# Depthwise taps of the second layer's conv branch: six per projection over the first seven heads, the rest handed out at the merges from the third on

## The chip, the core and the metric

The kernel runs on one core of a Trainium2 chip. Times are device microseconds of one execution. Engines are named as in the profile: PE is TensorE, DVE is VectorE, ACT is ScalarE, POOL is GpSimd, SP is SyncE, which issues the DMAs here.

## What is computed

Two layers of a hybrid block over 256 latent tokens and 256 context tokens, width 1024, in fp32. Of one layer, the part that matters here, with h the normalised and modulated input:

```
q, k, v = h @ w_q, h @ w_k, h @ w_v            # 8 heads, two 64-wide halves each; 2-D rotary on q and k
p   = softmax(q k^T / 8)                       # for each half, keys = context + latent (512)
o   = (p[0] - lam * p[1]) @ v
y_b = rms_norm(o, subln_g) * c @ w_attn_out    # per head
u   = (h @ w_a) * sigmoid(h @ w_b)             # 512 channels
u   = depthwise_conv(u, width 31) + bias
y_a = silu(layer_norm(u)) @ w_conv_out
y_c = group_mix(window_means(h @ w_p) - h @ w_p) @ w_pool_out
y   = (g0 * y_a + g1 * y_b + g2 * y_c) @ w_out     # g = sigmoid(h @ w_g + b), three branches
```

then the residual and a SwiGLU feed-forward part. The second layer's context rows are not needed, so there the queries, the conv branch and the pooling run for the 256 latent tokens alone, and keys and values for 512.

## The kernel before

Activations lie channel by channel, 128 channels on the partitions and the tokens along the row. Each fp32 product is three matmuls on TensorE (lines 341 to 343): high part times high part, low times high, high times low. The weights come in units of 128 x 1024; SP loads a unit (`raw`, line 305), ACT makes its high part (`hi`, line 357) and DVE its low part (`lo`, line 358). Activations are split likewise (H, V, A, QH and QL).

The program is written in one order, and a scheduler that models times decides from it in which order each engine gets its instructions; the written order serves as priority. The engines then run their own lists strictly in order and wait for each other by semaphores.

The second layer's token mixer, in the written order:

- `glu` computes u. `conv_tasks` then makes a list of 124 small tasks, `self.bg`, 31 for each chunk of 128 channels. For chunks 0, 1 and 2 they run on DVE: one start (line 909) and 30 taps, each a multiply-add of a shifted row of u into the chunk's sum, O (line 930, 128 x 241 to 255). For chunk 3 a tap is a multiplication on ACT (line 925) and an addition on POOL (line 927). A POOL task stands behind every third DVE tap.
- `step(n)` takes the next n tasks off the list and writes them at this point of the program; `drain()` writes all that are left.
- The first half of the V projection, then eight heads. For each head comes the projection of Q and that of K, each followed by `rope_split`: a copy out of PSUM to T on ACT (line 705), on DVE a shuffle into sh and a multiplication by the cosine (707, 708), on POOL the multiplication by the sine (710), on DVE the sum (711). For Q, four DMAs copy T to QD (line 731), and ACT and DVE split it (QH, QL). For K, ACT makes two copies (line 720) and POOL the two low parts (line 721). Behind each of the 16 projections stands a `step(16)`, so that the list was empty after the eighth.
- Behind a head's projections stand the scores and products of the head before it (`head`): score matmuls (line 800, into pss), the largest element on DVE (803), the exponential on ACT (806), the reciprocal and the difference of the two softmaxes on DVE (810 to 813), transposes on PE (831, into pst), the split into A (357 and 358), the products with V (into pso), a copy to O on ACT (844). Ahead of head 4 stands the second half of the V projection.
- Heads 0 to 3 go through `subln` in the loop, heads 4 to 7 behind it: squares on ACT (855), a mean on PE (856), a root on ACT (860), a reciprocal on DVE (861), a broadcast on PE (869, 870).
- Ahead of the second `subln` stand the pooling projections with `pool_group` on POOL (lines 1000 to 1022), behind it the merges: for each branch eight gate projections with the products of that branch, branch 1 (attention) first, then 2 (pooling), then 0 (conv). `norm` (lines 937 to 964), the layernorm over the four conv chunks, is put on the list ahead of the merges; its result is needed in the merges of branch 0 alone.

Of the kernel before, what the change touches and what calls it, by code (L numbers as in the profile page):

```python
# [38 lines left out]
NH = 8  # L39
# [173 lines left out]
class Net:  # L213
# [815 lines left out]
    def layer(self, l, H, acts, first, xin, xnext, tail):  # L1029
        nc = self.nc  # L1030
        need_ctx = l < DEPTH - 1
# [7 lines left out]
        def os_to_yb(h0, h1):  # L1039
            yb.extend(self.subln(os[h0:h1], sg, n))  # L1040
# [13 lines left out]
        for h in range(NH):  # L1054
            if h == 4:
                V1 = self.v_proj(l, 1, acts)
            qk = []
            for col, sc, m in ((COL_Q, HD ** -0.5, n), (COL_K, 1.0, NT)):
                u = self.unit("in", l, col + h * P)
                ps = self.ps("g")  # L1060
                self.gemm_cm(ps[:, :m], u, acts, 0, m)
                qk.append(self.rope_split(ps, sc, m, col == COL_K,
                                          nc.vector if need_ctx else nc.gpsimd))
                self.step(self.S_QK)
            if pend is not None:
                os.append(self.head(l, *pend, lam, need_ctx))
                if len(os) == 4:
                    os_to_yb(0, 4)
            pend = (h, qk[0], qk[1], V if h < 4 else V1)
            if h % 2 == 0 and fill:  # L1070
                self.mod_block(l, fill.popleft(), bank=self.H_BK)
        os.append(self.head(l, *pend, lam, need_ctx))

        if need_ctx:
            us = self.glu(l, acts, n)
            taps, norm = self.conv_tasks(l, us, nseq, ya)
        else:
            self.drain()


        pooled = []
# [11 lines left out]
        def merge(branch, n_, yact, u_y, base):  # L1093
            t = self.M_BK[n_ % 2]
            pg, py = self.ps(t), self.ps(t)
            u = self.unit("in", l, COL_G + branch * D + n_ * P)
            self.gemm_cm(pg[:, :n], u, acts, 0, n)
            u_y = self.unit(*u_y) if u_y is not None else self.last_u
            self.last_u = u_y
            self.gemm_cm(py[:, :n], u_y, yact, 0, n, base)  # L1100
            gs = self.c2("S")
            nc.scalar.activation(gs[:, :n], pg[:, :n], AF.Sigmoid,
                                 bias=prm[:, O_BG + branch * 8 + n_:
                                          O_BG + branch * 8 + n_ + 1])
            if branch == 1:
                m = self.cn("O", n)
                nc.vector.tensor_tensor(out=m[:, :n], in0=py[:, :n], in1=gs[:, :n],
                                        op=ALU.mult)
                ms.append(m)
            else:  # L1110
                m = ms[n_]
                nc.vector.tensor_tensor(out=gs[:, :n], in0=py[:, :n], in1=gs[:, :n],  # L1112
                                        op=ALU.mult)
                nc.gpsimd.tensor_tensor(out=m[:, :n], in0=m[:, :n], in1=gs[:, :n],  # L1114
                                        op=ALU.add)
            if branch == 0:
                hi, lo = self.pair("V", n)
                self.split(hi[:, :n], lo[:, :n], m[:, :n])
                mhl.append((hi[:, :n], lo[:, :n]))

        for n_ in range(KC):
            merge(1, n_, yb, ("ao", l, n_), 0)
            self.step(self.S_B)


        hi, lo = self.unit("grp", l)
# [262 lines left out]
```

## Time and profile before

| | before |
|---|---|
| three runs | 1535.64, 1538.06, 1538.65 us, median 1538.06 |
| the profiled execution's own time | 1536.55 us |
| its span | 1534.6 us |
| PE busy | 1498.8 us, 98% |
| DVE busy | 997.5 us, 65% |
| ACT busy | 821.0 us, 53% |
| POOL busy | 343.0 us, 22% |
| mean granted clock of TensorE | 0.992 of its higher level |

The span is the time between the first and the last instruction of the profiled execution; its own time is 2 us longer and lies 1.5 us under the median. Times in rows are counted from the start of the span; the second layer's heads lie between about 1035 and 1200.

### The profile page before, as it was taken

The numbers are of one execution on the slowest core, as the hardware profiler recorded it, in microseconds if no ns is written. First come the engines' busy times: TensorE is split into PE (matmuls) and PEld (weight loads), VectorE is DVE, ScalarE is ACT, GpSimd is POOL, SyncE is SP. The second block draws the span as 40 slices with busy tenths as digits, with TensorE's granted clock in tenths as the row PEclk, the third lists the DMA queues.
The fourth block names the chain that finished last, engine by engine and source line by source line (L and its number), as shares of the span: only waits on it lengthen the run. The fifth ranks groups of instructions, "written<-read, shape, count | busy, mean of one in ns | idle before, by whom it ended". The sixth has DMA issues, their size and how long they took to land.

```text
span 1534.6 us, 22266 instructions
## 1 busy us (share of the span) xinstructions
PE 1498.8 (98%) x8310; PEld 1250.9 (82%) x8310; DVE 997.5 (65%) x1561; ACT 821.0 (53%) x1383; POOL 343.0 (22%) x320
## 2 busy tenths in 40 slices
PE   6999999999999999999999999998999999899998
PEld 3788878878877787888888888887879899799986
DVE  4587786999974337344444332799999656655544
ACT  5467667532344336454545453774668665644443
POOL 0010100540131100054554543053225312000000
PEclk9999999999999999999999999999999999999999
DMA  9552342133237643335435667333143567366553
GB/s 350 183 155 73 124 138 69 70 105 115 98 102 243 213 147 110 124 125 178 165 127 173 208 210 253 130 118 122 58 145 109 176 202 242 125 196 209 182 189 110
DMA packets 85148, 236.68 MB, mean 154 GB/s; under 512 B 10032, under 2 KB 15792, under 8 KB 85040
## 3 DMA queue, kind: packets, MB, share of 16 engines
q1 hardware_dynamic: 85040, 235.26, 45.9%
q8 instruction: 65, 1.06, 0.3%
q14 instruction: 43, 0.35, 0.1%
HBM read 223.69 MB, written 5.24 MB: 149 GB/s over the span
## 4 chain that ended last, share of the span: by engine, by line
PE 83%; DVE 11%; ACT 3%; issue 2%; DMA 0%; SPq 0%; POOL 0%; DVEq 0%; ACTq 0%
PE psg L341 14%; PE psg L342 13%; PE psg L343 13%; PE pss L343 10%; PE pss L342 10%; PE pss L341 10%; DVE O L930 3%; PE pso L342 2%; PE pso L341 2%; PE pso L343 2%; DVE lo L358 2%; DVE Q L930 2%; PE pss L800 2%; PE pss L392 1%; PE pst L831 1%
## 5 line engine op out<-in xcount | busy, mean ns | idle before, releaser
L358 DVE TENSOR_TENSOR lo<-raw,hi 128x1024 fp32r<-128x1024 f32 x299 | 385.3, 1290 | 244.2 <-ACT hi L357 236.2
L357 ACT ACTIVATE hi<-raw 128x1024 fp32r<-128x1024 f32 x299 | 315.0, 1056 | 411.1 <-PE psg L342 165.7
L341 PE MATMUL psg<-H,hi 128*128 128x512 f32 (+1 forms) x864 | 300.6, 349 | 2.3 <-ACT H L357 1.9
L342 PE MATMUL psg<-H,hi 128*128 128x512 f32 (+1 forms) x864 | 300.7, 348 | 0.7 <-DVE H L358 0.7
L343 PE MATMUL psg<-H,lo 128*128 128x512 f32 (+1 forms) x864 | 300.9, 349 | 0.0
L341 PE MATMUL pss<-H,hi 128*128 128x256 f32 (+1 forms) x704 | 234.9, 335 | 2.9 <-ACT H L357 2.8
L343 PE MATMUL pss<-H,lo 128*128 128x256 f32 (+1 forms) x704 | 236.2, 336 | 0.0
L342 PE MATMUL pss<-H,hi 128*128 128x256 f32 (+1 forms) x704 | 235.7, 335 | 0.0
L473 POOL TENSOR_TENSOR ma<-ma,mt 128x512 f32<-128x512 f32 x91 | 133.2, 1481 | 246.8 <-ACT mt L469 245.7
L341 PEld LDWEIGHTS psg<-H,hi 128*128 128x128 f32 x864 | 163.5, 190 | 28.6 <-issue 3.7
L343 PEld LDWEIGHTS psg<-H,lo 128*128 128x128 f32 x864 | 163.7, 189 | 23.8 <-issue 2.9
L342 PEld LDWEIGHTS psg<-H,hi 128*128 128x128 f32 x864 | 163.7, 189 | 23.7 <-issue 1.9
L341 PEld LDWEIGHTS pss<-H,hi 128*128 128x128 f32 x704 | 132.8, 189 | 17.7 <-ACT H L357 3.0
L342 PEld LDWEIGHTS pss<-H,hi 128*128 128x128 f32 x704 | 133.3, 190 | 15.7 <-DVE H L358 0.2
L343 PEld LDWEIGHTS pss<-H,lo 128*128 128x128 f32 x704 | 134.1, 191 | 13.9
L930 DVE SCALAR_TENSOR_TENSOR Q<-Q,perm,Q 128x482 f32<-128x482 f32 (+14 forms) x120 | 99.0, 825 | 2.5
L710 POOL TENSOR_TENSOR sh<-sh,perm 128x256 f32<-128x256 f32 x32 | 27.8, 868 | 260.5 <-DVE sh L707 189.4
L1114 POOL TENSOR_TENSOR O<-O,S 128x512 f32<-128x512 f32 (+1 forms) x32 | 43.3, 1355 | 184.7 <-DVE S L1112 184.7
L806 ACT ACTIVATE E<-pss,st 128x512 f32<-128x512 f32 (+1 forms) x96 | 58.7, 613 | 36.1 <-DVE st L803 30.7
L469 ACT ACTIVATE mt<-mr,perm 128x512 f32<-128x512 f32 x91 | 61.6, 715 | 21.4 <-DMA mr<-wmod 21.4
L1182 DVE TENSOR_TENSOR S<-pss,S 128x256 f32<-128x256 f32 (+1 forms) x43 | 23.9, 555 | 74.2 <-PE pss L343 72.0
L341 PE MATMUL psg<-V,hi 128*128 128x512 f32 (+1 forms) x192 | 64.7, 342 | 1.2 <-ACT S L860 1.2
(388 smaller groups left out, 2773.3 us busy)
## 6 DMA issues: line engine op xcount, KB each, us to landing
raw<-w SPq DMA_DIRECT2D x297, 512.0 KB, 3.4
mr<-wmod SPq DMA_DIRECT2D x72, 256.0 KB, 4.2
mod<-wmod SPq DMA_DIRECT2D x24, 512.0 KB, 5.2
A<-wmod SPq DMA_DIRECT2D x18, 256.0 KB, 5.1
O<-wmod SPq DMA_DIRECT2D x16, 256.0 KB, 5.8
QD<-T SPq DMA_DIRECT2D x32, 128.0 KB, 2.4
E<-wmod SPq DMA_DIRECT2D x14, 256.0 KB, 5.4
xs<-Q SPq DMA_DIRECT2D x12, 256.0 KB, 2.0
```

Of the source, the lines that this page charges most:

```text
L341: mm(out, sh, mh, start=start, stop=False)
L342: mm(out, sh, ml, start=False, stop=False)
L343: return mm(out, sl, mh, start=False, stop=stop)
L357: return (self.nc.scalar.activation(hi, src, AF.Copy), (lo_eng or self.nc.vector).tensor_tensor(out=lo, in0=src, in1=hi.bitcast(F32), op=A ...
L358: (lo_eng or self.nc.vector).tensor_tensor(out=lo, in0=src, in1=hi.bitcast(F32), op=ALU.subtract))
L469: nc.scalar.activation(t, src, AF.Copy, scale=self.cc[:, k, v:v + 1])
L473: nc.gpsimd.tensor_tensor(out=accs[v], in0=accs[v], in1=t, op=ALU.add)
L710: nc.gpsimd.tensor_tensor(out=sh, in0=sh, in1=self.sin, op=ALU.mult)
L800: nc.tensor.matmul(pss[j][:, :n], q[a][:, j, qt * P:(qt + 1) * P], k[:, j, k0:NT], start=(a == 0), stop=(a == 1))
L806: nc.scalar.activation(e[:, :n], pss[j][:, :n], AF.Exp, bias=mx[:, j:j + 1], accum_out=ss[:, j:j + 1])
L930: last[0] = nc.vector.scalar_tensor_tensor(out=av, in0=uv, scalar=prm[:, w:w + 1], in1=av, op0=ALU.mult, op1=ALU.add)
L1114: nc.gpsimd.tensor_tensor(out=m[:, :n], in0=m[:, :n], in1=gs[:, :n], op=ALU.add)
```

## The change

In the second layer each of the fourteen projections of heads 0 to 6 is followed by six tasks instead of sixteen, and those of head 7 by none. The call that wrote the rest of the list behind the last head is removed. The 40 tasks that are then left are handed out, ten at a time, behind the merges of branch 1 from the third on, with `norm` behind them. The first layer's program stays as it was, since its list is empty in the loop over heads and all its merges keep their step.

```diff
--- before.py
+++ after.py
@@ -1061,7 +1061,7 @@
                 self.gemm_cm(ps[:, :m], u, acts, 0, m)
                 qk.append(self.rope_split(ps, sc, m, col == COL_K,
                                           nc.vector if need_ctx else nc.gpsimd))
-                self.step(self.S_QK)
+                self.step(6 if h < NH - 1 else 0)
             if pend is not None:
                 os.append(self.head(l, *pend, lam, need_ctx))
                 if len(os) == 4:
@@ -1074,8 +1074,6 @@
         if need_ctx:
             us = self.glu(l, acts, n)
             taps, norm = self.conv_tasks(l, us, nseq, ya)
-        else:
-            self.drain()
 
 
         pooled = []
@@ -1120,7 +1118,8 @@
 
         for n_ in range(KC):
             merge(1, n_, yb, ("ao", l, n_), 0)
-            self.step(self.S_B)
+            if need_ctx or n_ > 1:
+                self.step(self.S_B)
 
 
         hi, lo = self.unit("grp", l)
```

All instructions stay the same; what changes is the order on each engine. Up to the end of the chunk 0 taps every engine has the order it had, chunk 3's taps on POOL included; PE has it again within the merges. Three places in between:

DVE at head 0. O_9232 is the sum of chunk 1 in the kernel before; V_9020 and the lo tiles belong to the V projection and to coming weight units, sh_9065 and T_9063 to head 0's Q, sh_9135 and T_9133 to its K. Before:

```order
L358 TENSOR_TENSOR V_9020<-pso_8886,V_9019 128x512
L930 SCALAR_TENSOR_TENSOR O_9232<-O_8685,perm,O_9232 128x243
L358 TENSOR_TENSOR lo_8908<-raw_8905,hi_8907 128x1024
L707 STREAM_SHUFFLE sh_9065<-T_9063 128x256
L930 SCALAR_TENSOR_TENSOR O_9232<-O_8685,perm,O_9232 128x244
L708 TENSOR_TENSOR T_9063<-T_9063,perm 128x256
L930 SCALAR_TENSOR_TENSOR O_9232<-O_8685,perm,O_9232 128x245
L711 TENSOR_TENSOR T_9063<-T_9063,sh_9065 128x256
L930 SCALAR_TENSOR_TENSOR O_9232<-O_8685,perm,O_9232 128x246
```

with taps between the remaining steps of head 0's K as well. After, where sh_9121 and T_9119 are head 0's K:

```order
L358 TENSOR_TENSOR V_9020<-pso_8886,V_9019 128x512
L358 TENSOR_TENSOR lo_8908<-raw_8905,hi_8907 128x1024
L707 STREAM_SHUFFLE sh_9065<-T_9063 128x256
L708 TENSOR_TENSOR T_9063<-T_9063,perm 128x256
L711 TENSOR_TENSOR T_9063<-T_9063,sh_9065 128x256
L358 TENSOR_TENSOR lo_9035<-raw_9032,hi_9034 128x1024
L707 STREAM_SHUFFLE sh_9121<-T_9119 128x256
L708 TENSOR_TENSOR T_9119<-T_9119,perm 128x256
L711 TENSOR_TENSOR T_9119<-T_9119,sh_9121 128x256
L358 TENSOR_TENSOR lo_9091<-raw_9088,hi_9090 128x1024
```

The taps of chunk 1, thirteen instructions from behind the last chunk 0 tap to the last rotation step of head 0's K, are gone from this place; they stand together with the rest of their chain in the second V projection. 

DVE from the last head's softmax to the second `subln`'s reciprocal (line 861, the last row of each). A is the split of the transposed weights of the last heads. Before:

```order
L810 RECIPROCAL st_10661<-st_10647 128x2
L811 TENSOR_TENSOR st_10661<-st_10661,perm 128x1
L813 SCALAR_TENSOR_TENSOR E_10637<-E_10637,st_10642,E_10640 128x512
L358 TENSOR_TENSOR A_10601<-pst_10595,A_10600 128x512
L813 SCALAR_TENSOR_TENSOR E_10656<-E_10656,st_10661,E_10659 128x512
L358 TENSOR_TENSOR A_10616<-pst_10610,A_10615 128x512
L358 TENSOR_TENSOR lo_10935<-raw_10932,hi_10934 128x1024
L358 TENSOR_TENSOR A_10672<-pst_10666,A_10671 128x512
L358 TENSOR_TENSOR A_10687<-pst_10681,A_10686 128x512
L358 TENSOR_TENSOR E_10738<-A_10728,E_10738 128x256
L358 TENSOR_TENSOR lo_10965<-raw_10962,hi_10964 128x1024
L861 RECIPROCAL S_10895<-S_10895 128x256
```

After, where O_10334 is the sum of chunk 2:

```order
L813 SCALAR_TENSOR_TENSOR E_10596<-E_10596,st_10601,E_10599 128x512
L930 SCALAR_TENSOR_TENSOR O_10334<-O_8816,perm,O_10334 128x248
L930 SCALAR_TENSOR_TENSOR O_10334<-O_8816,perm,O_10334 128x247
L930 SCALAR_TENSOR_TENSOR O_10334<-O_8816,perm,O_10334 128x246
L358 TENSOR_TENSOR A_10612<-pst_10606,A_10611 128x512
L930 SCALAR_TENSOR_TENSOR O_10334<-O_8816,perm,O_10334 128x245
L358 TENSOR_TENSOR A_10627<-pst_10621,A_10626 128x512
L930 SCALAR_TENSOR_TENSOR O_10334<-O_8816,perm,O_10334 128x244
L930 SCALAR_TENSOR_TENSOR O_10334<-O_8816,perm,O_10334 128x243
L930 SCALAR_TENSOR_TENSOR O_10334<-O_8816,perm,O_10334 128x242
L930 SCALAR_TENSOR_TENSOR O_10334<-O_8816,perm,O_10334 128x241
L861 RECIPROCAL S_10835<-S_10835 128x256
```

Taps of chunk 2 now stand between these steps: of the chain's 31 instructions, 25 lie between the two reciprocals of line 861, 21 of them ahead of the last split of A, and the chain ends right ahead of the second reciprocal. Before, no tap stood between the two. Two lo splits stand behind the reciprocal now.

PE at the products of the last head (into pso; A is the split of its transposed weights, psg_11104 the gate projection of the first merge). Before:

```order
L342 MATMUL psg_11104<-H_8340,hi_10837 128x256
L343 MATMUL psg_11104<-H_8338,lo_10838 128x256
L341 MATMUL psg_11104<-H_8338,hi_10837 128x256
L342 MATMUL psg_11104<-H_8340,hi_10837 128x256
L341 MATMUL pso_10627<-A_10671,V_9914 128x256
L342 MATMUL pso_10627<-A_10672,V_9914 128x256
L343 MATMUL pso_10627<-A_10671,V_9915 128x256
L341 MATMUL pso_10627<-A_10671,V_9918 128x256
```

After:

```order
L831 MATMUL pst_10606<-perm,E_10577 128x128
L831 MATMUL pst_10606<-perm,E_10596 128x128
L831 MATMUL pst_10621<-perm,E_10596 128x128
L831 MATMUL pst_10621<-perm,E_10577 128x128
L831 MATMUL pst_10621<-perm,E_10596 128x128
L341 MATMUL pso_10567<-A_10611,V_9799 128x256
L342 MATMUL pso_10567<-A_10612,V_9799 128x256
L343 MATMUL pso_10567<-A_10611,V_9800 128x256
```

The matmuls of the first merge that stood between the last transposes (line 831) and these products are drawn ahead; the products now follow the transposes directly.

## Rows read from the trace of the kernel before

**Rows 1.** The page of the profile, its first line and the line of part 1 on PE (busy us, share of the span, instructions of each engine).

```profile
span 1534.6 us, 22266 instructions
...
PE 1498.8 (98%) x8310; PEld 1250.9 (82%) x8310; DVE 997.5 (65%) x1561; ACT 821.0 (53%) x1383; POOL 343.0 (22%) x320
```

**Rows 2.** Waits of PE from 1040 to 1215 us, the three longest: who waited for whom, then us in total, times, longest.

```profile
PE pss L800 <- POOL K L721: 5.2, 1, 5.2
PE pso L856 <- ACT sq L855: 1.4, 1, 1.4
PE psg L341 <- ACT S L860: 1.2, 1, 1.2
```

**Rows 3.** Windows over the second layer's attention part: start and end, length; busy us and (instructions) of PE, PEld, DVE, ACT, POOL; granted clock of TensorE as a share of its higher level; busy share of the DMA engines; GB/s.

```profile
1054.10:1060.90 6.80, 5.64 (x15) 4.65 (x16) 6.76 (x10) 4.51 (x6) 3.24 (x3) 0.50 0.25 84
1060.90:1190.00 129.10, 128.01 (x759) 109.44 (x758) 124.60 (x238) 91.48 (x179) 45.78 (x52) 1.00 0.33 107
1197.50:1200.90 3.40, 3.40 (x17) 2.95 (x16) 2.39 (x4) 2.36 (x5) 0.00 (x0) 0.50 0.93 311
1220.00:1240.00 20.00, 20.00 (x167) 19.95 (x167) 13.73 (x20) 18.20 (x29) 0.00 (x0) 1.00 0.73 230
```

**Rows 4.** Timeline of PE ahead of the first score matmul: start, length, engine, line, operation, out<-in, count. The starts of neighbours show the pitch.

```profile
1049.71 0.28 PE L341 MATMUL psg<-H,hi 128*128 128x256 f32 x1
1049.83 0.28 PE L342 MATMUL psg<-H,hi 128*128 128x256 f32 x1
```

**Rows 5.** Timeline of DVE in the first V projection and at head 0 (and one row from the second V projection); several instructions of one kind in a row are one row with their count.

```profile
1019.40 3.15 DVE L930 SCALAR_TENSOR_TENSOR O<-O,perm,O 128x255 f32<-128x255 f32 x4
...
1035.84 0.93 DVE L930 SCALAR_TENSOR_TENSOR O<-O,perm,O 128x241 f32<-128x241 f32 x1
...
1038.02 0.45 DVE L930 SCALAR_TENSOR_TENSOR O<-O,perm,O 128x241 f32<-128x241 f32 x1
1038.40 1.21 DVE L358 TENSOR_TENSOR lo<-raw,hi 128x1024 fp32r<-128x1024 f32 x1
...
1042.04 0.43 DVE L707 STREAM_SHUFFLE sh<-T 128x256 f32<-128x256 f32 x1
...
1045.33 2.78 DVE L930 SCALAR_TENSOR_TENSOR O<-O,perm,O 128x246 f32<-128x246 f32 x4
...
1049.56 0.45 DVE L707 STREAM_SHUFFLE sh<-T 128x256 f32<-128x256 f32 x1
...
1052.67 0.41 DVE L711 TENSOR_TENSOR T<-T,sh 128x256 f32<-128x256 f32 x1
...
1100.93 3.57 DVE L930 SCALAR_TENSOR_TENSOR O<-O,perm,O 128x249 f32<-128x249 f32 x7
```

**Rows 6.** Timeline of POOL at head 0; in brackets the idle time ahead of the row and who ended it.

```profile
1042.55 0.87 POOL L710 TENSOR_TENSOR sh<-sh,perm 128x256 f32<-128x256 f32 x1 [5.21 <-DVE sh L707]
1043.39 3.42 POOL L927 TENSOR_TENSOR O<-O,mt 128x244 f32<-128x244 f32 x4
...
1053.89 2.73 POOL L721 TENSOR_TENSOR K<-T,K 64x512 fp32r<-64x512 f32 x2 [2.95 <-ACT K L720]
```

**Rows 7.** Timeline of ACT at head 0: the copy of head 0's K out of PSUM, the split of head 0's Q, the copies of its K.

```profile
1040.01 0.58 ACT L705 ACTIVATE T<-psg 128x512 f32<-128x512 f32 x1
...
1049.63 0.63 ACT L357 ACTIVATE QH<-QD 128x512 fp32r<-128x512 f32 x1 [6.27 <-DMA QD<-T]
1053.18 1.28 ACT L720 ACTIVATE K<-T 64x512 fp32r<-64x512 f32 x2 [2.92 <-DVE T L711]
```

**Rows 8.** Windows from the end of the chunk 0 taps to the second `subln` (columns as in rows 3), with the sum over all four windows asked for.

```profile
1036.70:1147.40 110.70, 104.46 (x545) 86.07 (x544) 109.57 (x212) 65.97 (x125) 33.63 (x31) 0.97 0.34 107
...
1149.10:1189.90 40.80, 40.80 (x296) 37.91 (x295) 37.39 (x65) 33.27 (x67) 20.73 (x31) 1.00 0.33 108
1189.90:1197.15 7.25, 4.67 (x36) 3.43 (x34) 1.75 (x3) 3.71 (x7) 6.82 (x9) 1.00 0.04 14
sum 160.45, PE 151.62 PEld 129.02 DVE 150.41 ACT 104.63 POOL 61.49; mean PE 37.91 PEld 32.26 DVE 37.60 ACT 26.16 POOL 15.37
```

**Rows 9.** The same windows, line 930 (the taps on DVE) alone: start and end, length, busy us of DVE and (instructions), clock, DMA share, GB/s.

```profile
1036.70:1147.40 110.70, 33.02 (x61) 0.97 0.34 107
1149.10:1189.90 40.80, 0.00 (x0) 1.00 0.33 108
```

**Rows 10.** Timeline of DVE: the reciprocal of the first `subln`, the last split of A, the reciprocal of the second `subln`.

```profile
1149.12 1.75 DVE L861 RECIPROCAL S<-S 128x256 f32<-128x256 f32 x1
...
1189.20 0.69 DVE L358 TENSOR_TENSOR A<-pst,A 128x512 fp32r<-128x512 f32 x1 [0.70 <-ACT A L357]
...
1197.15 1.75 DVE L861 RECIPROCAL S<-S 128x256 f32<-128x256 f32 x1 [0.76 <-ACT S L860]
```

**Rows 11.** Timeline of ACT ahead of the second `subln`'s reciprocal: the copy of the last head's output, the root.

```profile
1193.39 0.39 ACT L844 ACTIVATE O<-pso 128x256 f32<-128x256 f32 x1 [3.92 <-PE pso L343]
...
1196.64 0.47 ACT L860 ACTIVATE S<-pso,perm 128x256 f32<-128x256 f32 x1
```

**Rows 12.** Timeline of POOL in `pool_group`, two rows of line 1007 with the same form.

```profile
1180.22 1.69 POOL L1007 TENSOR_TENSOR A<-A 128x269 f32<-128x269 f32 x1
...
1184.56 0.63 POOL L1007 TENSOR_TENSOR A<-A 128x269 f32<-128x269 f32 x1
```

**Rows 13.** The first matmul of the conv layernorm in the second layer: engine, count, ns least/median/most, first and last start.

```profile
L943 PE MATMUL pso<-row,perm x2: 377/378/378, 1209.2 to 1209.4; 128*128 128x256 f32 x2
```

## Prediction

> **What bounds the kernel now.** I read the page's totals first [rows 1]: PE is busy for 98% of the span, so a gain can only come from the few microseconds in which PE stands still or runs at half clock. The list of PE's waits over the second layer's heads [rows 2] says how few: 5.2 us at the first score matmul (line 800), waiting for K on POOL, and 1.4 and 1.2 us around the second `subln`. The windows by clock [rows 3] show what follows such waits. From 1054.1 to 1060.9, behind the first, the granted clock is 0.50 (1.2 GHz); in the whole of 1060.9 to 1190 it is 1.00 (2.4 GHz); from 1197.5 to 1200.9, behind the other two, it is 0.50 again. Half the clock does half the work, so the first stretch costs 6.8 / 2 = 3.4 us and the second 3.4 / 2 = 1.7. All that an order of the work can win here is thus 5.2 + 3.4 at the first score and 2.6 + 1.7 at the end of the heads.
>
> **Why PE waits at the first score.** The chain is read on three engines. DVE finishes the tap chain of channel chunk 0 at 0.79 us for a tap while POOL runs its own chain (3.15 us for four), ends it at 1036.77, goes on with chunk 1's, and reaches the shuffle of head 0's Q only at 1042.04, that of head 0's K at 1049.56 and K's last rotation step (line 711) at 1052.67 [rows 5]. POOL idles 5.21 us until the first shuffle, does the rotation's multiplication (line 710), then the last four taps of its own chain until 1046.8, and splits K from 1053.89 on [rows 6]. ACT had K's input ready at 1040.6, hence K is 9 us late at its shuffle because of DVE's queue alone [rows 7].
>
> **The change at the first stall.** By the order, thirteen chunk-1 instructions leave the place ahead of K's rotation on DVE, and everything between them stays. From 1036.77 I put the remaining DVE work end to end: V split 0.60, lo 1.13 (that at 1038.40, less its overlap [rows 5]), V 0.60, lo 1.14, shuffle 0.34, then line 708, POOL's line 710 (0.87) and line 711. Head 0's Q is rotated near 1042.0 instead of 1045.3. Its transfer to QD (line 731) let the split QH start at 1049.63 before [rows 7], some 4.2 us behind the rotation; now about 1046.3. K's shuffle comes near 1044, but POOL works through its four taps first (3.42 us [rows 6]), so line 710 for K runs to about 1045.9 and line 711 to 1046.3. K's two ACT copies stand behind QH, 1046.9 to 1048.2 (1.28 [rows 7]), and POOL's first half of the K split is done at about 1049.0, its second, with a line 710 between, near 1051. PE arrives eight matmuls earlier, 1049.95 − 8 × 0.12 = 1049.0 [rows 4]. So most of the 5.15 us goes; I leave 0.8 for the second half. Saved: 4.4 us. From 1060.9 to 1190 PE stood still for 1.1 us in all, in pieces, without a drop of the clock [rows 3], so I let the half-clock stretch go too: 3.4 more. **First stall: about 7.8 us earlier.** Bounds: nothing, if POOL's four taps or the QD transfer keep K where it is; 8.6 if the whole wait goes.
>
> **What the middle pays.** Chunk 1's 31 instructions now stand in the stretch of the second V projection. Before, seven taps ran back to back there in 3.57 us, 0.51 each, with POOL quiet [rows 5]. That stretch is bound by PE, and DVE's room in it grows as the taps leave the front, so I cost it at nothing. If the cover were missing, 31 × 0.51 = 16 us would stand on DVE, which idled for only 1.1 us from 1036.7 to 1147.4 [rows 8]; but 33.02 us of its work there was taps [rows 9], of which 25 leave the stretch altogether.
>
> **What the last heads pay.** Here the change costs. Between the first `subln` reciprocal at 1149.12 and the last split of A, which ends at 1189.89 [rows 10], DVE was busy for 37.39 of 40.8 us with no tap [rows 8, 9]; with 7.8 us taken off and DVE less late, that stretch starts near 1140. The order of the change puts 25 taps of chunk 2 between the two reciprocals, 21 of them ahead of the last A split. What does one cost there? Alone it takes 0.385 (1038.02 to 1038.40 [rows 5]). The mean of all 61 from 1036.7 to 1147.4 is 33.02 / 61 = 0.54, with POOL busy 33.63 / 110.7 = 30% of that time; in the last heads POOL is busy 20.73 / 40.8 = 51% [rows 8]. On a straight line through the first two points, 0.385 + 0.155 × 51 / 30 = 0.65. So 21 × 0.65 = 13.7 us. Bounds: 21 × 0.46 = 9.7, if each costs what the profile shows for a single tap, and 21 × 0.79 = 16.6, the price beside POOL's taps. The last A split then ends near 1140 + 37.4 + 13.7 = 1191.1 (1187 to 1194).
>
> From the last A split to the second reciprocal before took 1197.15 − 1189.89 = 7.3 us, with DVE busy for only 1.75 of it [rows 8, 10]: PE had other matmuls in front of the last head's products. In the changed order PE goes from the transposes straight to these products (about 0.6), and from the start of the O copy to the end of the root it is 1197.11 − 1193.39 = 3.7 us [rows 11], in which ACT also did another split: 4.0 in all. The four taps behind the last A split lie under it. **Second reciprocal: 1191.1 + 4.0 = 1195.1 against 1197.15, 2 us earlier.** From there PE is full (20.00 of 20 us from 1220 [rows 3]), so what is gained there is gained at the end.
>
> A balance says the same. DVE idles 160.45 − 150.41 = 10.0 us from 1036.7 to 1197.15 [rows 8], and its work is the same in both kernels. If the middle leaves 6 us idle and the tail 2.5, 1 to 2 us remain as gain.
>
> The price of a tap is where I chose. The trace shows the contention from both sides: a DVE tap takes 0.79 beside POOL's taps against 0.385 alone [rows 5], and POOL's line 1007 takes 1.69 beside DVE's work at 1180.22 against 0.63 at 1184.56 [rows 12]. The Trainium skill, "SBUF — State Buffer", section "Who interferes with whom", says that a VectorE instruction with two SBUF inputs contends with a GpSimd instruction that reads SBUF, and that where the shared ports are taken, whoever issues first has them for the whole instruction while the other fully blocks. The trace agrees with it in size. By that rule a tap there can wait for a whole line 1007, and an estimate for all of them is 21 × (0.385 + 0.63) = 21.3 us in place of 13.7. It speaks against the change, on the side of rival C.
>
> The conv layernorm (`norm`, lines 937 to 964) needs chunk 2's last tap, now right ahead of the second reciprocal; its first matmul stood at 1209.2 [rows 13], 12 us behind that reciprocal. Three POOL additions fit into that, so it costs nothing; without that cover, some 3 us. The hand-out at the merges moves no tap behind the last head: by the order none is left there.
>
> **Rivals.** *A, my forecast (0.42):* the first stall's 7.8 us are won and the taps in the last heads give 4 to 8 of them back: 0 to 4 earlier, 1532.5 to 1536.5 on the profile's own time. *B, the gain is kept (0.25):* taps there cost 0.46 or fall into the 3.4 us that DVE idled, so 9.7 us or less instead of 13.7, and with a shorter stand at the tail the second half-clock stretch (1.7) goes: 5 to 9 earlier, 1528 to 1531. Against it: POOL's half share. *C, slower by the taps (0.15):* each waits for a whole POOL instruction, 0.85 to 1.0 a tap, 18 to 21 us; the reciprocal comes at 1199.3 to 1202.5, 2 to 5 later: 1539 to 1542. It decides from (1197.15 − 1140 − 37.4 − 4.0) / 21 = 0.75 a tap on. *D, the first stall stays (0.13):* K still waits, for POOL's four taps or the QD transfer, DVE has no taps to do meanwhile, and the last heads pay all the same: with the first reciprocal at 1145 to 1149, 3 to 7 later, 1539 to 1543. It decides where less than about 5.5 us are won at the stall.
>
> **How the numbers follow.** The profile's own time is 1536.55 around a span of 1534.6; the median of the three runs, 1538.06, is 1.5 above it. The gain of 2 from the first gives 1534.5, from the median 1536.1; I say 1535.5. The range takes in A, most of B and the nearer half of C and D: 1529 to 1541. 0.2% is 3.1 us, about what a measurement of this kernel can tell from no change. Faster by more than that: B and the upper part of A, 0.36. Slower: the farther halves of C and D and a stall elsewhere, 0.20. The rest, 0.44.
>
> **What would show it.** Right: PE's wait at the first score under 1.5 us, and no half clock behind it; the first reciprocal of `subln` near 1140; taps from there to the last A split at a mean near 0.65; that split near 1191, PE straight behind it; the second reciprocal near 1195. Wrong: a wait at line 800 of 3 us or more (D); a tap mean under 0.5 (B) or over 0.75 (C); a stall of PE between 1060 and 1140 (the middle isn't free); a conv layernorm that PE waits for near 1209.

## The result and the profile after

The changed kernel takes 1544.91 us in the median of five runs against 1537.91: a ratio of 1.0055, 95% interval 1.0043 to 1.0066. It is 7 to 8.5 us slower; 2 us faster, no measurable change, was forecast, with 1541 as the upper end of the range. A few executions in the rounds of the experiments, of a run or of the kernel before, fell in a slow state (1832 to 2101 us); all medians leave them out.

The page of the changed kernel, its first line and the line on busy times:

```profile
span 1545.2 us, 22282 instructions
...
PE 1502.5 (97%) x8310; PEld 1252.1 (81%) x8310; DVE 998.6 (65%) x1561; ACT 821.9 (53%) x1383; POOL 341.5 (22%) x320
```

The profiled execution took 1547.0 us, the slowest of the five. Of the 10.6 us between its span and that of [rows 1], 2.1 were there before the change begins: the last tap of chunk 0, up to which all orders are the same, starts at 1037.94 instead of 1035.84 [rows 5], and it is already there, 2.0 us, at the fortieth instruction of DVE. So 8.5 us lie behind it, as the ratio says. "Net" means below: less this offset of each trace.

PE's waits in the second layer, to be held against [rows 2]:

```profile
PE pst L831 <- DVE E L813: 4.4, 2, 3.6
PE psg L341 <- ACT V L357: 3.3, 1, 3.3
PE pss L800 <- POOL K L721: 2.4, 4, 1.0
PE pst L869 <- ACT row L357: 1.9, 1, 1.9
PE psg L341 <- ACT V L1002: 1.6, 1, 1.6
PE pso L342 <- DVE A L358: 1.2, 1, 1.2
PE pso L856 <- ACT sq L855: 0.9, 1, 0.9
```

The reader is to see that the 5.2 us for head 0's K have become four waits of 2.4 us together, two for head 0 (1.6) and two for head 1 (0.7). The second `subln` has two waits as before, 1.9 and 0.9 us instead of 1.2 and 1.4. The rest is new or was short before: 4.4 and 1.2 us for the last heads' softmax and splits on DVE, 1.6 for a copy of the pooling branch, and 3.3 for a split V on ACT, which lies among the merges.

DVE's timeline at the places of [rows 5, 10]:

```profile
1037.94 0.93 DVE L930 SCALAR_TENSOR_TENSOR O<-O,perm,O 128x241 f32<-128x241 f32 x1
...
1146.29 1.73 DVE L861 RECIPROCAL S<-S 128x256 f32<-128x256 f32 x1
...
1195.06 0.68 DVE L358 TENSOR_TENSOR A<-pst,A 128x512 fp32r<-128x512 f32 x1
1195.66 0.92 DVE L930 SCALAR_TENSOR_TENSOR O<-O,perm,O 128x245 f32<-128x245 f32 x1
1196.50 0.68 DVE L358 TENSOR_TENSOR A<-pst,A 128x512 fp32r<-128x512 f32 x1
...
1202.50 1.75 DVE L861 RECIPROCAL S<-S 128x256 f32<-128x256 f32 x1 [3.42 <-ACT S L860]
```

The first reciprocal of `subln` comes at 1146.29 (net 1144.2; 1149.1 before), the last split of A ends at 1197.1 (net 1195.0; 1189.9), the second reciprocal comes at 1202.50 (net 1200.4; 1197.15).

Windows of the same stretches, columns as in [rows 3], and line 930, the taps, alone in the fourth, columns as in [rows 9]:

```profile
1038.80:1090.00 51.20, 47.92 (x249) 39.56 (x248) 45.75 (x83) 33.35 (x64) 22.85 (x21) 1.00 0.40 123
1090.00:1120.00 30.00, 30.00 (x171) 26.08 (x170) 29.50 (x59) 16.39 (x29) 0.93 (x2) 1.00 0.30 93
1120.00:1146.30 26.30, 26.30 (x146) 21.19 (x145) 24.16 (x48) 18.53 (x33) 9.93 (x9) 1.00 0.38 115
1146.30:1197.10 50.80, 44.32 (x312) 40.40 (x310) 50.73 (x89) 34.24 (x70) 24.38 (x34) 0.96 0.32 105
1197.10:1202.50 5.40, 4.48 (x25) 2.74 (x25) 1.88 (x6) 2.58 (x5) 3.11 (x5) 0.76 0.00 0
```

```profile
1146.30:1197.10 50.80, 13.67 (x21) 0.96 0.32 105
```

DVE idles 5.5, 0.5 and 2.1 us in the first three, 8.1 in all, and hardly at all between the first reciprocal and the last split of A (50.73 of 50.80). The 21 taps there take 13.67 us.

Both traces hold the same 8310 matmuls, so the start of the n-th tells how far PE is ahead, wherever the order differs little. The table gives these differences to the kernel before, net, in us, for the changed kernel and for the experiments below; the last column is the timed difference of the medians. Each is against the executions of the kernel before that were timed in the same rounds. The timed column holds the rest of the program as well, whose time varies between executions by some microseconds (1533.8 to 1540.8 for the kernel before), while the other columns are of one execution each.

| | 5160th, behind head 0's first scores | 5580th, ahead of the last heads | 5880th, last head | 6090th, behind the second `subln` | 6390th, among the merges | 8000th | timed |
|---|---|---|---|---|---|---|---|
| changed kernel | −5.8 | −5.6 | −4.2 | +4.7 | +9.7 | +8.5 | +7.0 |
| six, with drain | −6.5 | −4.8 | −3.4 | +4.0 | +4.0 | +3.7 | +2.8 |
| layernorm late | +0.1 | +0.1 | +0.1 | +1.6 | +6.6 | +5.2 | +5.0 |
| no third edit | −6.5 | −4.8 | −3.4 | +5.2 | +5.2 | +4.5 | +3.2 |
| no late taps | −5.8 | −5.5 | −5.9 | −4.7 | −4.7 | −5.2 | −7.9 |
| seven, with drain | −6.4 | −5.5 | +0.1 | +6.6 | +6.6 | +5.2 | +4.5 |
| chunk 1 behind head 0's K | −5.8 | −4.7 | −5.5 | −3.9 | −2.2 | −3.0 | −2.6 |
| chunk 1 behind head 1's K | −5.8 | −5.4 | −6.4 | +4.2 | +4.2 | +3.7 | +3.8 |
| layernorm one merge earlier | +0.2 | 0.0 | 0.0 | +1.7 | +3.4 | +2.1 | +0.9 |
| chunk 1 behind head 0's K, twelve tasks | −4.2 | −4.6 | −3.1 | −0.5 | −0.5 | −1.4 | −1.1 |

Read along the first line, the change wins 5.8 us at the first stall, loses 1.6 up to the last head, 8.9 from there to behind the second `subln`, and 5.0 among the merges; 1.2 come back later. The clock has its part in the two large losses:

```profile
1195.00:1200.00 5.00, 4.02 (x17) 2.69 (x17) 3.97 (x8) 0.15 (x1) 2.08 (x4) 0.53 0.00 0
...
1205.00:1210.00 5.00, 4.89 (x27) 4.57 (x27) 2.22 (x7) 1.34 (x4) 0.00 (x0) 0.66 0.02 3
...
1245.00:1250.00 5.00, 2.23 (x19) 2.02 (x17) 2.18 (x4) 5.00 (x11) 0.00 (x0) 1.00 0.58 196
1250.00:1255.00 5.00, 4.51 (x25) 4.51 (x26) 4.13 (x8) 4.97 (x11) 0.00 (x0) 0.66 0.73 249
```

From 1195 to 1200 the granted clock is 0.53, from 1205 to 1210 it is 0.66, and behind the stand in 1245 to 1250 (2.23 us busy of 5) it is 0.66 again, where the kernel before, at its merges from 1220 to 1240, ran at 1.00 [rows 3]. The 1.2 us that come back lie near 1345, where the half-clock stretch is shorter than in the kernel before, whose row is the first:

```profile
1337.40:1344.20 6.80, 6.45 (x29) 6.23 (x30) 4.74 (x7) 3.98 (x8) 0.00 (x0) 0.50 0.18 66
```

```profile
1349.90:1353.30 3.40, 3.18 (x16) 3.05 (x15) 3.00 (x6) 3.40 (x7) 0.00 (x0) 0.50 0.00 0
```

The short stretch is also found in runs without a late layernorm (seven, with drain), so it is no gain that this edit is shown to bring.

### The profile page after: what moved, and what is told of

It is laid out like the page before. It is cut to its first block, busy times and chain, and to the rows that moved or that the text cites. A ratio compares the mean times of both kernels' runs of the same rounds, so it can differ in the third digit from the quotient of the medians.

```text
span 1545.2 us, 22282 instructions
## 1 busy us (share of the span) xinstructions
PE 1502.5 (97%) x8310; PEld 1252.1 (81%) x8310; DVE 998.6 (65%) x1561; ACT 821.9 (53%) x1383; POOL 341.5 (22%) x320
## 4 chain that ended last, share of the span: by engine, by line
PE 86%; DVE 6%; ACT 4%; DMA 2%; issue 1%; SPq 0%; POOL 0%; DVEq 0%; ACTq 0%; POOLq 0%
PE psg L341 14%; PE psg L342 14%; PE psg L343 14%; PE pss L343 10%; PE pss L342 10%; PE pss L341 9%; PE pso L342 3%; PE pso L343 3%; PE pso L341 3%; PE pss L800 2%; DVE Q L930 1%; DVE lo L358 1%; PE pss L392 1%; PE pst L831 1%; ACT hi L357 1%
```

## Experiments

**The spread alone.** The first of the three edits, with the drain and the merges' steps as they were:

```diff
-                self.step(self.S_QK)
+                self.step(6 if h < NH - 1 else 0)
```

> Only the first of the three edits: six tasks per projection over heads 0 to 6, the rest written behind the last head, the conv layernorm handed out behind the first merge as in the kernel before. Theory S (two separate causes: the taps in the last heads make the second subln late, and the late hand-out of the layernorm costs a second stall among the merges): the front and the tail are those of the changed kernel, the stall near 1250 is gone; 3 to 5 us slower than before, 1541 to 1543. Rival T (one cause: the late end of the taps makes the layernorm late by itself, so the second stall stays): about 7 us slower, 1545.

Measured: ratio 1.0019 (1.0010 to 1.0028), 1539.96 us. PE's four longest waits in this run:

```profile
PE pst L831 <- DVE E L813: 4.4, 2, 3.6
PE pss L800 <- POOL K L721: 2.8, 4, 1.6
PE psg L341 <- ACT V L1002: 1.6, 1, 1.6
PE pso L342 <- DVE A L358: 1.0, 1, 1.0
```

The waits at the last heads are nearly those of the changed kernel; that of 3.3 us for V is gone. By the traces the two kernels have the same order on every engine up to the layernorm's second matmul and the rows around it. In the table the run keeps its +4.0 from the second `subln` to the merges, where the changed kernel loses another 5.0. So there are two causes.

**The late layernorm alone.** All taps as before, `norm` taken off the list behind the seventh merge, as in the changed kernel:

```diff
-            self.step(self.S_B)
+            if need_ctx or n_ > 5:
+                self.step(self.S_B)
```

> The kernel before with the layernorm alone handed out later, behind the seventh merge of branch 1; all taps stay where they were. Theory S: the second layernorm matmul stands 77 matmuls later, PE waits 3 us or more for the split of the pooling branch's output (V on ACT) and runs at half clock behind it; 3 to 5 us slower than before, 1541 to 1543. Rival T: the layernorm has slack of 12 us, so nothing changes, 1538.

Measured: ratio 1.0027 (1.0018 to 1.0035), 1542.12 us. Of PE's waits, two rows:

```profile
PE pss L800 <- POOL K L721: 5.2, 1, 5.2
PE psg L341 <- ACT V L357: 3.3, 1, 3.3
```

The stall at head 0 is that of the kernel before, and the 3.3 us for V are there with no tap moved. In the table the run goes from +1.6 to +6.6 at the merges, the same 5.0 us as the changed kernel. The 1.6 ahead of it come with the half-clock stretch behind the second `subln`, which lasts 6.8 us here instead of 3.4 [rows 3]:

```profile
1197.40:1204.20 6.80, 6.80 (x33) 6.32 (x32) 4.17 (x8) 3.45 (x8) 0.00 (x0) 0.50 0.67 229
```

By the traces the order up to there is the same on every engine, so they are no part of the edit. The two runs' timed losses add up to 7.8 us, the changed kernel has 7.0.

**The third edit taken back.** Drain removed, tasks handed out from the first merge on, so that `norm` comes behind the fifth merge instead of the seventh:

```diff
-            if need_ctx or n_ > 1:
-                self.step(self.S_B)
+            self.step(self.S_B)
```

> The first two edits without the third: the drain is gone, but the rest of the tasks is handed out from the first merge on, so the layernorm comes behind the fifth merge instead of the seventh. By the order its second matmul stands at 5666 on PE (5744 in the changed kernel, 5667 before) and all taps stand as in the changed kernel. Theory S: the stall of 3.3 us and its half-clock stretch near 1245 are gone, the tail stays: 3 to 4 us slower than before, as with the first edit alone. Rival: the missing drain costs by itself, 6 us slower or more.

Measured: ratio 1.0021 (1.0012 to 1.0031). The list of PE's waits has none for V on line 357. Without the third edit the order is that of "the spread alone" on every engine but for two neighbouring matmuls, by the traces, so the removed drain moves nothing and costs nothing; it is the two merges' delay that pushes `norm` too far.

**One merge earlier.** As "layernorm late" with `n_ >= 5`, so behind the sixth merge.

> The kernel before with the layernorm handed out behind the sixth merge of branch 1 (the run with the seventh merge was 4 us slower). By the order its second matmul moves by 29 matmuls on PE, 3.5 us, against 77. Theory S: the block of ACT work behind it ends about 4 us later than before instead of 11, still ahead of the pooling branch's copies of T that PE needs: no change, 1536 to 1538. Rival V (any shift of the layernorm costs in proportion): 1.5 to 2 us slower.

Measured: ratio 1.0009 (1.0000 to 1.0019). Of PE's waits:

```profile
PE psg L341 <- ACT V L357: 1.4, 1, 1.4
```

Theory S expected no wait here and falls on this point: with 29 matmuls' delay the wait is already 1.4 us, with 77 it is 3.3. It is a matter of degree, nearer to rival V; the timed 0.9 us, with an interval down to nothing, does not decide between them. PE is 1.7 us behind at the 6270th matmul, by a longer half-clock stretch as in "layernorm late", and 3.4 at the 6300th, which is the wait and little more; with the full delay the half-clock stretch behind the longer wait is added.

**The taps of the last heads left out.** As "the spread alone", but the last 26 taps of chunk 2 are missing, so the convolution is not complete:

```diff
-                tasks.append(tap(i, d))
+                tasks.append(tap(i, d) if nseq == 2 or i < 2 or d < 5 else lambda: None)
```

> As with six tasks and the drain, but the last 26 taps of channel chunk 2 in the second layer are left out (work is missing), so no tap stands between the two reciprocals of subln. Theory S (the taps there are the cause of the tail): the 4 to 6 us won at the first score carry to the end, 4 to 7 us faster than before, 1531 to 1534. Rival T (the tail is late because PE has spent its filler matmuls, or because POOL is late): still 2 us slower or more, 1540.

Measured: ratio 0.9947 (0.9932 to 0.9963). The window over the last heads, columns as in [rows 3]:

```profile
1150.00:1185.00 35.00, 35.00 (x276) 33.23 (x275) 31.43 (x54) 28.00 (x56) 21.30 (x33) 1.00 0.36 114
```

Without the taps DVE idles 3.6 us there, PE not at all, and of the 5.8 us won at the front 4.7 are left behind the second `subln` and 5.2 at the 8000th matmul. (This trace was 1.9 us ahead before the orders part, which the table takes off.) The last split of A ends 10.2 us earlier, net, than in "the spread alone". The rival's filler matmuls are not separated by this run, since PE's order changed with the taps: 14 matmuls of a gate projection stand again between the last transposes and the last head's products (1181.95 to 1183.60), as in the kernel before. What speaks against it is DVE, which the taps kept full up to the last split of A (50.73 of 50.80 us in the changed kernel), and that the tail behind that split took 4.9 us here and 5.3 with the taps. What POOL does to the price of a tap is not separated either.

**Seven instead of six.** `self.step(7 if h < NH - 1 else 0)`, drain as before.

> Seven instead of six tasks per projection over heads 0 to 6, the rest written behind the last head, layernorm as before. By the order 16 instead of 21 taps then stand between the first reciprocal of subln and the last split of A. Theory S (each tap there costs 0.65 of DVE's time, and DVE bounds that stretch): 5 taps less are 3 us less than with six and the drain, so 0 to 2 us slower than before, 1538 to 1540. Rival T (the stretch is bound by something else, POOL's pool_group or ACT): as slow as with six.

Measured: ratio 1.0024 (1.0015 to 1.0032), no better than six. Theory S is wrong in where DVE's idle time ends:

```profile
1130.00:1150.00 20.00, 20.00 (x105) 15.64 (x104) 20.00 (x42) 15.02 (x28) 5.68 (x5) 1.00 0.34 106
1150.00:1165.00 15.00, 13.19 (x87) 11.13 (x86) 15.00 (x30) 10.16 (x19) 4.20 (x11) 0.95 0.43 141
1165.00:1175.00 10.00, 10.00 (x79) 10.00 (x78) 10.00 (x23) 8.36 (x19) 1.15 (x1) 0.91 0.27 79
1175.00:1185.00 10.00, 9.55 (x74) 8.84 (x72) 10.00 (x13) 6.59 (x13) 9.07 (x9) 1.00 0.32 107
```

DVE is full from 1130 on, not only from the first reciprocal at 1145. Of the nine taps that left the stretch behind that reciprocal, five of them from ahead of the last split of A, eight went into 1120 to 1145. The last split of A came only 0.5 us earlier for it, net, than with six tasks, and the second reciprocal 0.5 later. What seems to count is how many tap instructions are done before DVE fills up, by about 1120 net: 31 with six tasks, 33 with seven, 56 before. Rival T is not excluded by this run: PE's waits are others than with six, among them 3.0 us for the exponential (line 806) and 2.5 for a sigmoid of the merges, both on ACT, and DVE idles 1.5 us behind 1185.

**Chunk 1 behind head 0's K.** The kernel before with one edge in the order of DVE, `rot` being the instruction of line 711:

```diff
-                    self.after(last[0], ins)
+                    self.after(last[0] if nseq == 2 or i != 1 else self.rk, ins)
...
+                if h == 0 and col == COL_K:
+                    self.rk = self.rot
                 self.step(self.S_QK)
```

> The kernel before (16 tasks per projection, drain, layernorm as before) with one more edge in the order of DVE: chunk 1's first instruction stands behind head 0's last rotation step of K. By the order no tap is ahead of that step, ten taps are in heads 0 and 1, and 7 stand between the two reciprocals of subln (25 with six tasks and the drain, 16 with seven). Theory S (the front's gain is real and is lost where DVE has no idle time left, from about 1120 on; what counts is how many taps are done by then): the front's 5 to 6 us are won and most is kept, 2 to 5 us faster than before, 1533 to 1536. Rival U (any departure from the old tap order costs the tail its filler matmuls): as slow as with six and the drain, 1540.

Measured: 1533.83 against 1536.40 us, ratio 0.9978 (0.9970 to 0.9987): faster than both kernels. DVE by stretch and the taps alone, columns as above:

```profile
1036.70:1060.00 23.30, 21.61 (x120) 18.34 (x119) 21.23 (x39) 12.03 (x20) 10.39 (x11) 1.00 0.48 151
1060.00:1090.00 30.00, 29.09 (x148) 24.07 (x147) 30.00 (x63) 21.20 (x44) 12.44 (x10) 1.00 0.28 89
1090.00:1120.00 30.00, 27.91 (x164) 23.75 (x164) 29.57 (x60) 18.36 (x34) 1.71 (x2) 1.00 0.36 114
1120.00:1150.00 30.00, 30.00 (x158) 23.71 (x157) 29.87 (x57) 20.53 (x36) 9.86 (x16) 1.00 0.32 99
```

```profile
1036.70:1060.00 23.30, 5.29 (x10) 1.00 0.48 151
...
1150.00:1200.00 50.00, 0.00 (x0) 0.97 0.29 95
```

Ten taps run in 1036.7 to 1060, behind head 0's K; DVE idles 2.6 us up to 1150 where the changed kernel idled 8.1, 47 tap instructions are done by 1120, and no tap is left behind 1150. The second reciprocal comes at a net 1193.3.

**Chunk 1 behind head 1's K**, with ten tasks per projection in heads 0 and 1.

> As the run with chunk 1 behind head 0's K, but the edge is set behind head 1's K, and 10 tasks are handed out per projection in heads 0 and 1. By the order 11 taps stand between the two reciprocals of subln. Theory S: a little less is kept, 0 to 3 us faster than before, 1535 to 1538; the waits of PE for the K of head 1 (0.2 to 1.6 us with six tasks) go. Rival U: 1540.

Measured: ratio 1.0023 (1.0014 to 1.0032): slower by 3.8 us, where Theory S expected 0 to 3 faster. 41 tap instructions were done by 1120, and eight taps ran behind 1150; they are enough to take 10.6 us between the 5880th and the 6090th matmul. The sign fits "done by 1120", the size does not: between 41 and 47 there is a jump of 8 us in the table, which a price per tap can't explain. PE stands still in one piece there and runs at half clock behind it, as in the changed kernel; why so few taps decide it stays open.

**Chunk 1 behind head 0's K, twelve tasks per projection.**

> Chunk 1 behind head 0's K, and 12 instead of 16 tasks per projection. The taps on DVE stand as with 16, but the layernorm's second matmul stands at 5668 on PE instead of 5687. Theory S: the wait of 1.4 us near 1243 that was left with 16 goes, the rest stays: 4 to 6 us faster than before, 1531 to 1533. Rival: that wait had another cause, and it is as with 16 tasks, 3 us faster.

Measured: ratio 0.9996 (0.9987 to 1.0006). The wait for V (1.4 us with sixteen, at 1236.9 in that trace) is gone from PE's list, as Theory S said, and the table's difference stays level from the second `subln` (−0.5) through the merges (−0.5); but 3.4 us fewer were kept up to there than with sixteen. In this run the mean clock from 1036.7 to 1060 was 0.93 and from 1190 to 1195 it was 0.52, against 1.00 and 0.75 with sixteen. What sets these stretches off wasn't tried.

## Why the prediction was wrong, step by step

Forecast were 2 us less, measured are 8.5 more, net. Of the 10.5 between, 5.3 came by the second reciprocal of `subln`, some 1.5 by the half clock behind it, 5.0 by the conv layernorm, and 1.2 came back near 1345.

- **The first stall** was right in its mechanism and too large by 2 us. Forecast were 7.8 us, the 5160th matmul shows 5.8. The half-clock stretch is gone, as argued. But I left 0.8 us for one second half of K, and PE waits 1.6 us for the two halves of head 0's. And I counted the stretch's 6.8 us whole, though it begins within the wait: PE is busy for only 5.64 of them [rows 3], so the half clock cost 2.8 us, not 3.4. The last 0.6 of the 2 I can't place. With two more waits for head 1's K 5.6 us are left by the 5580th matmul.
- **The middle** cost PE nothing, as forecast. But I assumed that the lead would reach the first reciprocal enlarged, at 1140; the extra 1.3 us had no number behind them. It came at a net 1144.2, 4.9 earlier than before, since DVE had idled 8.1 us by then, not the 6 of my balance, and was full from 1135 on (11.30 of 11.30 us).
- **The last heads**: the price of a tap was right. 21 taps were forecast at 0.65, 13.7 us; the trace has 13.67, with POOL busy for 24.38 of 50.80 us, about the share that I had put in. One stretch is one point; it does not show the straight line elsewhere. DVE's 37.4 and these make 51.1, and the stretch took 50.8. The Trainium skill's rule on the shared ports ("SBUF — State Buffer", "Who interferes with whom") describes this contention, but the worst case that I worked out by it, a whole POOL instruction per tap (21.3 us), did not come. Seen against the run without the taps, they cost 10.2 us of time; the rest of their price went into time in which DVE idles without them (3.6 us from 1150 to 1185 in that run). The balance that was to confirm the sum failed on its premise that DVE's work is the same in both kernels: up to the second reciprocal it took 152.0 us instead of 150.4, and DVE idled 11.7 us instead of 10.0.
- **The tail** was forecast at 4.0 us from the last split of A to the reciprocal and took 5.4. Two rows of ACT show where:

```profile
1199.85 0.38 ACT L844 ACTIVATE O<-pso 128x256 f32<-128x256 f32 x1 [5.30 <-PE pso L343]
...
1201.99 0.47 ACT L860 ACTIVATE S<-pso,perm 128x256 f32<-128x256 f32 x1
```

  From the end of the last split of A (1197.18) to the copy of O it took 2.7 us where I had put 0.6: PE's last products ran at half clock, with six matmuls of line 856 (1.07 us) among them. From the copy to the reciprocal it was 2.65, less than the 3.4 that I had put. I had kept the clock behind PE's stand at the last head out of the sum. The second reciprocal came 3.2 us later than before instead of 2 earlier, 5.3 in all, 4.2 by the late start and 1.4 by the tail, less 0.3 in the stretch between; a half-clock stretch of 3.4 us then cost up to 1.7 more, so that PE is 4.7 behind. The kernel before has such a stretch too, but there it lay mostly ahead of the matmuls that wait for the reciprocal (lines 869 and 870), and here behind them.
- **The conv layernorm at nothing is the step that failed outright**: it cost 5.0 us. I looked at its first matmul (line 943), which hardly moves, from the 6017th place on PE to the 6020th, and stopped there. Its second (line 960) moves from the 6110th to the 6187th (places in the traces, as in the table; the numbers in the expectations are 443 lower throughout), so PE's order is not the old one again within the merges, as I had it in the section on the change. It moves because `norm` is written behind the seventh merge instead of the first and the written order is the priority; behind the fifth it did not move ("no third edit"). With it moves a block of ACT work, as the two timelines of ACT show, the kernel before first (line 1134 there is line 1133 in the changed kernel):

```profile
1219.66 1.28 ACT L961 ACT_TABLE_LOAD   x1
1221.17 0.47 ACT L961 ACTIVATE row<-pso,perm 128x256 f32<-128x256 f32 x1 [0.23 <-PE pso L960]
...
1225.60 1.28 ACT L967 ACT_TABLE_LOAD   x1
...
1237.30 1.18 ACT L1134 ACTIVATE T<-psg,perm 128x256 f32<-128x256 f32 x3
```

```profile
1237.73 1.28 ACT L961 ACT_TABLE_LOAD   x1
1239.02 0.47 ACT L961 ACTIVATE row<-pso,perm 128x256 f32<-128x256 f32 x1
...
1242.82 1.28 ACT L967 ACT_TABLE_LOAD   x1
...
1246.67 0.46 ACT L1133 ACTIVATE T<-psg,perm 128x256 f32<-128x256 f32 x1
...
1250.03 0.41 ACT L357 ACTIVATE V<-T 128x256 fp32r<-128x256 f32 x1
```

  Before, the block from the root (line 961) to the silu (967) lay at 1219.66 to 1230, and the pooling branch's copies T, from which V is split for the next matmuls, came at 1237.30, seven us behind it. After, the block begins at 1237.73, T comes at 1246.67, with rows of the silu between the copies, and the first V at 1250.03: PE waits 3.3 us for it and then runs at half clock for about 3.4. Among the block's rows are loads of a function table of 1.28 us each, and the next activation starts 1.29 us after the load begins (1237.73 to 1239.02). The Trainium skill ("ScalarE: Activation LUTs", "What ACT_TABLE_LOAD costs") gives about 2.66 us for such a switch, a drain of the engine included; this trace shows half of it, and the measurement decides.
- Of the rivals, C came nearest in its outcome, but not by its mechanism: it wanted over 0.75 us a tap. D was nearer in mechanism: 5.8 us were won at the stall where it wanted less than about 5.5, DVE idled without taps at the front, and the second reciprocal came 3.2 us late (D: 3 to 7). No rival had the layernorm. That the hand-out at the merges moves no tap behind the last head was right, and beside the point.

## What to carry to other kernels

Where a list of small tasks is handed out later, follow the last task on it, and all its steps on every engine up to the one that somebody waits for, not only its first. Filler work moved out of a stall must land where its engine is idle: count that engine's idle time by stretch, and treat the whole stretch up to the next idle time as one queue; moving work inside it gained nothing here (seven tasks against six). The smallest edit that removes the stall, one edge that lets head 0's K pass the taps, gained 2.6 us where the spread over seven heads alone lost 2.8, and with the late layernorm 7.0.

## What was not expected of the hardware

With the same order on every engine up to that place, the half-clock stretches around the second `subln` differed between traces: the two runs with the layernorm alone moved were 1.6 and 1.7 us behind the kernel before at the 6090th matmul, with a stretch of 6.8 us instead of 3.4 [rows 3] and no edit ahead of it. "The spread alone" and "no third edit", whose orders are the same up to there, stood at +4.0 and +5.2. Each kernel has one trace, so differences of 1 to 2 us at this place are not to be read as effects of an edit. What starts and ends these stretches was not tried.
